# Wider opening tiles in the feed-forward phases, norms spread over three engines, and conv taps in another order, in a two-block transformer kernel

## The chip, the cores and the metric

The kernel runs on one core of a Trainium2 chip. The metric is the device time of one launch in microseconds (us), the median of several runs; less is better. The engines are named as in the profile: PE (TensorE matmuls; PEld its weight loads), DVE (VectorE), ACT (ScalarE), POOL (GpSimd) and SP (SyncE, which issues the transfers of weights).

## The reference, cut to what matters

Two models run one after the other on the same 256 tokens of width 1024, in fp32. Each has two layers.

```python
# first block, two layers
h = rms_norm(x, norm_mix_w);  z = h @ w_in + b_in
...                           # dilated attention, mLSTM, gates
x = x + mixed @ w_out
x = x + jnp.square(jax.nn.relu(rms_norm(x, norm_mlp_w) @ w_ff1)) @ w_ff2
# then a final rms_norm, then the second block, two layers
x = x + 0.5 * rmsnorm(swiglu_ffn(rmsnorm(x, ffn1_pre_g), ffn1_w_gu, ffn1_w_down), ffn1_post_g)
x = x + rmsnorm(mixing_sublayer(rmsnorm(x, mix_pre_g), ...), mix_post_g)
x = x + 0.5 * rmsnorm(swiglu_ffn(rmsnorm(x, ffn2_pre_g), ffn2_w_gu, ffn2_w_down), ffn2_post_g)

def rmsnorm(x, g):            # over 1024 columns
    return x * lax.rsqrt(jnp.mean(x * x, -1, keepdims=True) + EPS) * g
def swiglu_ffn(h, w_gu, w_down):
    a, b = jnp.split(h @ w_gu, 2, axis=-1)
    return (jax.nn.silu(a) * b) @ w_down
```

The mixing sublayer of the second block has four branches. Two matter here: a causal convolution over 256 channels with 31 taps and a layer norm behind it (the mean over channels comes out of a matmul), and a sparse attention that keeps the 64 best keys of each query.

## The kernel before, in words

**Phases.** The program is a list of steps in ten phases: mix1, ff, mix1, ff (first block; ff is the relu feed-forward), then f1, mix2, f2, f1, mix2, f2 (second block; f1 and f2 are the silu feed-forwards). The 256 tokens are two halves of 128, called token 0 and token 1 (`t`).

**Products.** Every fp32 operand is split into a high and a low part, and each product is three matmuls (high by high, high by low, low by high), all recorded on line 184. Weights come in tiles of 1 MB: SP issues the transfer (L210), ACT casts the high part (L224, two halves), DVE subtracts for the low part (L233, two halves), and PE multiplies. Three raw tiles, five high and four low ones can be in flight. A step uses one tile, 12288 columns of moving operand. Where weights are the stationary operand, matmuls are 512 and 256 columns wide (the low part of the tokens is joined by L348 on ACT and L349 on DVE, which free the PSUM bank); where tokens are stationary they are as wide as the tile's columns. PSUM has four banks for such products (`wk`) and four for the rest (`acc`).

**Seams.** Between two phases (`seam`) the norm of token 0 is made while token 1 still runs its last steps, and the norm of token 1 while token 0 opens the next phase. At such a place ACT squares the two 512-column halves with a sum each (L469), POOL makes the reciprocal root in three operations (L462, L463, and the power L464), DVE scales (L477), PE transposes (L358), and ACT and DVE split the result (L301, L302). Where a phase ends with a norm of its own (f1, mix2, f2: `post_residual`) there are two such chains in a row: squares of the sums in PSUM, POOL, then on DVE `y = acc * r * w` (L503) and `x = 0.5 * y + x` (L505) or `x = y + x` (L507) for each half, and then the norm that the next phase begins with.

**Openings.** A feed-forward phase opens with tokens as the stationary operand, so that token 0 can start before token 1: with relu three blocks of 256 columns for each token, with silu two blocks, each a pair of 256-column tiles (`start`), all over the full depth of 1024. The products of a block are transposed later (`tail`). The other blocks (`full`) have weights as the stationary operand.

**Side work.** The branches of mix2 are generators. After each step every generator goes on to its next `yield`. A scheduler orders each engine's queue at build time by priority and modelled readiness: the conv has low priority (−60), norms have high priority (120).

Of the kernel before, what the change touches and what calls it, by code (L numbers as in the profile page):

```python
# [12 lines left out]
AF = mybir.ActivationFunctionType  # L13
OP = mybir.AluOpType
# [3 lines left out]
P = 128  # L18
# [104 lines left out]
class Net:  # L123
# [334 lines left out]
    def rstd_halves(self, ss):  # L458

        nc = self.nc  # L460
        m0, m1, r = self.tiny(1), self.tiny(1), self.tiny(1)
        nc.gpsimd.tensor_scalar(out=m0, in0=ss[0], scalar1=1.0 / D, scalar2=EPS, op0=OP.mult, op1=OP.add)  # L462
        nc.gpsimd.tensor_scalar(out=m1, in0=ss[1], scalar1=1.0 / D, scalar2=m0, op0=OP.mult, op1=OP.add)  # L463
        nc.gpsimd.tensor_tensor(out=r, in0=m1, in1=self.mhalf[:, 0:1], op=OP.pow)  # L464
        return r

    def square(self, junk, src):
        ss = self.tiny(1)
        self.nc.scalar.activation(junk, src, AF.Square, accum_out=ss)  # L469
        return ss  # L470
# [26 lines left out]
    def post_residual(self, t, accs, w, half):  # L497

        nc = self.nc
        y = self.slot([P, D])  # L500
        r = self.rstd_halves([self.square(y[:, cs], accs[t][h]) for h, cs in enumerate(HALF)])
        for h, cs in enumerate(HALF):
            nc.vector.scalar_tensor_tensor(out=y[:, cs], in0=accs[t][h], scalar=r, in1=w[:, cs], op0=OP.mult, op1=OP.mult)  # L503
            if half:
                nc.vector.scalar_tensor_tensor(out=self.x[t][:, cs], in0=y[:, cs], scalar=0.5, in1=self.x[t][:, cs], op0=OP.mult, op1=OP.add)  # L505
            else:
                nc.vector.tensor_add(self.x[t][:, cs], y[:, cs], self.x[t][:, cs])  # L507

# [98 lines left out]

    def ff_plan(self, tag, w1, w2, kind, head):

        nc = self.nc  # L610
        n = (D_FF if kind == "relu" else D_FF_2) // 256
        nw = 1 if kind == "relu" else 2
        act, held = {}, {}
# [8 lines left out]
        def first_tiles(i):  # L622
            if kind == "relu":
                return (self.w_tile(w1, i * 256),)
            return (self.w_tile(w1, i * 256), self.w_tile(w1, D_FF_2 + i * 256))

        def tail(i, t, g):
            def gen():
                b = self.bank([P, 2, P])
                for k in range(2):  # L630
                    self.turn(b[:, k, :], g[:, k * P : (k + 1) * P])
                ts = tok(t)
                self.split(act[i].his(0, ts), act[i].los(0, ts), b)
                return
                yield
            return gen()

        def start(i, t, j):
            def fn(w):
                if i not in act:  # L640
                    act[i] = XT(self, 2)
                if j == 0:
                    held[t] = self.bank([P, nw, 256])
                b = held[t]
                self.a_mm([b[:, j, :]], self.xt, 0, t, w, 8, True, True, 256)
                self.flush()
                if j < nw - 1:
                    return
                g = self.slot([P, 2, 256])
                if kind == "relu":  # L650
                    nc.scalar.activation(g[:, 0, :], b[:, 0, :], AF.Relu)
                    nc.vector.tensor_mul(g[:, 1, :], g[:, 0, :], g[:, 0, :])
                else:
                    nc.scalar.activation(g[:, 0, :], b[:, 0, :], AF.Silu)
                    nc.vector.tensor_mul(g[:, 1, :], b[:, 1, :], g[:, 0, :])
                self.late.append(tail(i, t, g[:, 1, :]))
            return fn
# [29 lines left out]

        tiles = [first_tiles(i) for i in range(head)]
        starts = [[(start(i, t, j), (tiles[i][j],)) for i in range(head) for j in range(nw)] for t in range(2)]
        ntail = TAIL  # L690
# [375 lines left out]
    def mix2_plan(self, l):  # L1066
# [125 lines left out]
        def conv():  # L1192
            pt, hb = st["pt"], st["hb"]
            cv = self.half([P, 2, T])
            n = 0
            for c in range(2):
                for k in range(CONV_K):
                    w = pt[:, 2 * k + c : 2 * k + c + 1]
# [5 lines left out]
                    if n % TAPS == 0:  # L1204
                        yield
            yield
            b = self.acc([P, T])
# [54 lines left out]
        def sparse():  # L1262
# [3 lines left out]
            for t in (1, 0):  # L1266
# [130 lines left out]
    def plan(self):  # L1397
# [10 lines left out]
        def make(kind, l):  # L1408
            if kind == "mix1":
                return self.mix1_plan(l)  # L1410
            if kind == "ff":
                return (None, *self.ff_plan("ff", a["w_ff1"][l], a["w_ff2"][l], "relu", 3))
# [3 lines left out]
            return (None, *self.ff_plan(kind, a[f"{n}_w_gu_2"][l], a[f"{n}_w_down_2"][l], "silu", 2))  # L1416

# [114 lines left out]
```

## Time and profile before

| | before |
|---|---|
| time, median of 3 runs | 2001.76 us (2001.09 to 2002.98) |
| profiled execution, its own time | 2001.08 us |
| its span | 1999.3 us |
| mean granted TensorE clock in it | 0.994 |
| PE busy | 1944.3 us (97%) |
| DVE busy | 1321.1 us (66%) |
| ACT busy | 1029.2 us (51%) |
| POOL busy | 63.6 us (3%) |

The span is what the trace shows; the time of the run has 1.8 us around it. PE is busy nearly all the time, so a change is worth what it takes from PE's own work and from the few places at which PE waits.

### The profile page before, as it was taken

Reading aid. Unit: us, or ns where it says so; the run is one execution under the profiler, and the core shown is the slowest. Engines: PE = TensorE matmul, PEld = TensorE weight load, DVE = VectorE, ACT = ScalarE, POOL = GpSimd, SP = SyncE. Lnnn points to the kernel's source line nnn. Section 1 sums busy time; section 2 is a strip of 40 time slices with the busy share of each in tenths; the row PEclk is TensorE's granted clock in tenths of the full one; section 3 lists DMA queues with packets and bytes.
Section 4 is the critical chain, followed back from the end, with each engine's and each line's share of the span. In section 5 each row is a group of like instructions: output and inputs, shape, how many; then the busy total and the mean of one; then the engine's idle time right before and its main releaser. Section 6 shows DMA issues by size and latency. Waiting matters only on the chain.

```text
span 1999.3 us, 27988 instructions
## 1 busy us (share of the span) xinstructions
PE 1944.3 (97%) x11208; PEld 1687.3 (84%) x11208; DVE 1321.1 (66%) x2070; ACT 1029.2 (51%) x1694; POOL 63.6 (3%) x147
## 2 busy tenths in 40 slices
PE   7999999999999999999999999999999999999998
PEld 5888888888888888988798888888888798888887
DVE  5866666577666656655669777556655669777554
ACT  5555444455645444555555455555555555455552
POOL 0000000000000000000100000000000100000000
PEclk8999999999999999999999999999999999999999
DMA  8554565555445565556555455555556444546551
GB/s 282 164 175 140 166 209 190 190 191 174 142 158 181 189 196 175 196 189 213 162 153 160 157 179 201 190 198 177 191 188 214 154 148 154 162 174 206 190 194 70
DMA packets 252911, 356.97 MB, mean 179 GB/s; under 512 B 9399, under 2 KB 206188, under 8 KB 252780
## 3 DMA queue, kind: packets, MB, share of 16 engines
q1 hardware_dynamic: 252780, 355.17, 53.9%
q8 instruction: 88, 1.44, 0.3%
q14 instruction: 43, 0.35, 0.1%
HBM read 353.31 MB, written 1.84 MB: 178 GB/s over the span
## 4 chain that ended last, share of the span: by engine, by line
PE 86%; DVE 6%; ACT 3%; issue 2%; POOL 1%; DMA 1%; SPq 0%; POOLq 0%; DVEq 0%; ACTq 0%
PE wk L184 51%; PE acc L184 30%; DVE lo L233 2%; PE wk L358 1%; ACT slot L469 1%; ACT hi L224 1%; PE acc L358 1%; DVE half L1202 1%; DVE slot L477 1%; DMA raw<-in_w_in_dram 1%; DVE slot L503 1%; POOL tiny L464 1%; DMA raw<-in_w_ff_dram 1%; POOL tiny L463 1%; PE acc L834 0%
## 5 line engine op out<-in xcount | busy, mean ns | idle before, releaser
L184 PE MATMUL wk<-slot,hi 128*128 128x512 f32 (+1 forms) x3424 | 1022.3, 363 | 3.0 <-ACT slot L301 3.0
L233 DVE TENSOR_TENSOR lo<-raw,hi 128x1024 fp32r<-128x1024 f32 (+1 forms) x646 | 775.7, 1218 | 303.6 <-PE wk L184 212.1
L224 ACT CAST hi<-raw 128x1024 fp32r<-128x1024 f32 (+1 forms) x646 | 651.6, 1049 | 290.6 <-PE acc L184 114.2
L184 PE MATMUL wk<-slot,lo 128*128 128x256 f32 x2880 | 763.7, 282 | 0.0
L184 PEld LDWEIGHTS wk<-slot,hi 128*128 128x128 f32 x3424 | 597.7, 190 | 87.4 <-ACT slot L301 3.4
L184 PE MATMUL acc<-hi,slot 128*128 128x512 f32 x1920 | 617.0, 394 | 3.4 <-ACT slot L301 2.2
L184 PEld LDWEIGHTS wk<-slot,lo 128*128 128x128 f32 x2880 | 547.6, 190 | 24.7
L184 PEld LDWEIGHTS acc<-hi,slot 128*128 128x128 f32 x1920 | 362.3, 189 | 80.0 <-ACT slot L301 2.9
L184 PE MATMUL acc<-lo,slot 128*128 128x512 f32 x960 | 377.4, 393 | 0.0
L184 PEld LDWEIGHTS acc<-lo,slot 128*128 128x128 f32 x960 | 181.5, 189 | 37.3
L348 ACT COPY slot<-wk 128x256 f32<-128x256 f32 x196 | 73.2, 374 | 268.1 <-PE wk L184 267.7
L349 DVE TENSOR_TENSOR slot<-wk,slot 128x256 f32<-128x256 f32 x196 | 82.7, 422 | 106.8 <-ACT slot L348 106.8
L184 PE MATMUL wk<-hi,slot 128*128 128x256 f32 x704 | 134.6, 288 | 5.4 <-DVE slot L302 3.9
L184 PEld LDWEIGHTS wk<-hi,slot 128*128 128x128 f32 x704 | 111.3, 191 | 8.6 <-DVE slot L302 5.7
L184 PE MATMUL wk<-lo,slot 128*128 128x256 f32 x352 | 99.2, 283 | 0.0
L348 ACT COPY half<-wk 128x256 f32<-128x256 f32 x96 | 35.5, 370 | 87.0 <-PE wk L184 86.8
L302 DVE TENSOR_TENSOR slot<-slot 128x512 fp32r<-128x512 f32 x62 | 42.9, 692 | 41.3 <-ACT slot L301 41.3
L301 ACT CAST slot<-wk 128x256 fp32r<-128x256 f32 x108 | 38.0, 374 | 58.6 <-PE wk L358 50.1
L184 PEld LDWEIGHTS wk<-lo,slot 128*128 128x128 f32 x352 | 67.3, 191 | 0.2
L301 ACT CAST slot<-slot 128x512 fp32r<-128x512 f32 x62 | 38.6, 623 | 51.0 <-DVE slot L674 31.3
L358 PE MATMUL wk<-ident,slot 128*128 128x128 f32 x216 | 39.9, 281 | 19.7 <-DVE slot L477 12.9
L1202 DVE SCALAR_TENSOR_TENSOR half<-slot,prmT,half 128x256 f32<-128x256 f32 x120 | 57.3, 483 | 0.2
(238 smaller groups left out, 1040.2 us busy)
## 6 DMA issues: line engine op xcount, KB each, us to landing
raw<-in_w_in_dram SPq DMA_DIRECT2D x90, 1024.0 KB
raw<-in_ffn_w_gu_dram SPq DMA_DIRECT2D x88, 1024.0 KB
raw<-in_w_ff_dram SPq DMA_DIRECT2D x64, 1024.0 KB
raw<-in_ffn_w_down_dram SPq DMA_DIRECT2D x44, 1024.0 KB
raw<-in_w_out_dram SPq DMA_DIRECT2D x16, 1024.0 KB
raw<-in_w_branch_dram SPq DMA_DIRECT2D x8, 1024.0 KB
raw<-in_w_proj_att_dram SPq DMA_DIRECT2D x4, 1024.0 KB
raw<-in_w_proj_mlstm_dram SPq DMA_DIRECT2D x4, 1024.0 KB
```

Source lines behind the costliest of these rows:

```text
L184: i = self.nc.tensor.matmul(*args, **kwargs)
L224: nc.scalar.copy(his[j][:, p], raw[j][:, p])
L233: nc.vector.tensor_sub(lo[:, p], r[:, p], hi[:, p].bitcast(F32))
L301: nc.scalar.copy(hi, src)
L302: nc.vector.tensor_sub(lo, src, hi.bitcast(F32))
L348: self.nc.scalar.copy(dst, b[:, 1, :])
L349: self.nc.vector.tensor_add(dst, b[:, 0, :], dst)
L358: self.nc.tensor.transpose(dst, src, self.ident[: src.shape[0], : src.shape[0]])
L463: nc.gpsimd.tensor_scalar(out=m1, in0=ss[1], scalar1=1.0 / D, scalar2=m0, op0=OP.mult, op1=OP.add)
L464: nc.gpsimd.tensor_tensor(out=r, in0=m1, in1=self.mhalf[:, 0:1], op=OP.pow)
L469: self.nc.scalar.activation(junk, src, AF.Square, accum_out=ss)
L1202: nc.vector.scalar_tensor_tensor(out=cv[:, c, :], in0=hb[:, c, k : k + T], scalar=w, in1=cv[:, c, :], op0=OP.mult, op1=OP.add)
```

## The change

Five things change. The feed-forward phases open with tiles of 512 columns and half the depth (two groups of two such tiles for each token; with relu that is four blocks of 256, one more than before; with silu each tile holds 256 columns of both matrices, loaded by two transfers). In `rstd_halves` DVE makes the first sum, ACT the second, and POOL only the power; the squares carry the factor 1/1024 as a scale of 1/32. In `post_residual` the weight, and the 0.5, are multiplied in before `r` is known, and `x = y * r + x` is all that follows it; the squares write to a buffer of their own. The conv's taps alternate its two channel blocks, and there is one more yield behind them. The sparse attention has one more yield behind its exponentials.

```diff
     def rstd_halves(self, ss):
-        nc.gpsimd.tensor_scalar(out=m0, in0=ss[0], scalar1=1.0 / D, scalar2=EPS, op0=OP.mult, op1=OP.add)
-        nc.gpsimd.tensor_scalar(out=m1, in0=ss[1], scalar1=1.0 / D, scalar2=m0, op0=OP.mult, op1=OP.add)
+        nc.vector.tensor_scalar(out=m0, in0=ss[0], scalar1=EPS, scalar2=None, op0=OP.add)
+        nc.scalar.activation(m1, ss[1], AF.Identity, bias=m0)
         nc.gpsimd.tensor_tensor(out=r, in0=m1, in1=self.mhalf[:, 0:1], op=OP.pow)
     def square(self, junk, src):
-        self.nc.scalar.activation(junk, src, AF.Square, accum_out=ss)
+        self.nc.scalar.activation(junk, src, AF.Square, scale=1.0 / 32.0, accum_out=ss)
     def post_residual(self, t, accs, w, half):
-        y = self.slot([P, D])
-        r = self.rstd_halves([self.square(y[:, cs], accs[t][h]) for h, cs in enumerate(HALF)])
+        y, junk = self.slot([P, D]), self.slot([P, D])
+        ss = []
         for h, cs in enumerate(HALF):
-            nc.vector.scalar_tensor_tensor(out=y[:, cs], in0=accs[t][h], scalar=r, in1=w[:, cs], op0=OP.mult, op1=OP.mult)
-            if half:
-                nc.vector.scalar_tensor_tensor(out=self.x[t][:, cs], in0=y[:, cs], scalar=0.5, in1=self.x[t][:, cs], op0=OP.mult, op1=OP.add)
-            else:
-                nc.vector.tensor_add(self.x[t][:, cs], y[:, cs], self.x[t][:, cs])
+            ss.append(self.square(junk[:, cs], accs[t][h]))
+            nc.vector.scalar_tensor_tensor(out=y[:, cs], in0=accs[t][h], scalar=0.5 if half else 1.0, in1=w[:, cs], op0=OP.mult, op1=OP.mult)
+        r = self.rstd_halves(ss)
+        for h, cs in enumerate(HALF):
+            nc.vector.scalar_tensor_tensor(out=self.x[t][:, cs], in0=y[:, cs], scalar=r, in1=self.x[t][:, cs], op0=OP.mult, op1=OP.add)
     def ff_plan(self, tag, w1, w2, kind):
+        nw, per = (1, 2) if kind == "relu" else (2, 1)
+        head = 2 * per
+        def start_tile(i, half):
+            if kind == "relu":
+                return self.z_tile(w1, i * 512, half)
+            rows = w1[half * 512 : half * 512 + 512]
+            loads = []
+            for j, c in enumerate((i * 256, D_FF_2 + i * 256)):
+                loads.append((lambda r, j=j: r[:, :, j * 256 : (j + 1) * 256], rows[:, c : c + 256].rearrange("(k p) n -> p k n", p=P)))
+            return self.weight([P, 4, 512], *loads)
...
-                if j == 0:
-                    held[t] = self.bank([P, nw, 256])
+                if half == 0:
+                    held[t] = self.bank([P, 512])
                 b = held[t]
-                self.a_mm([b[:, j, :]], self.xt, 0, t, w, 8, True, True, 256)
+                self.a_mm([b], self.xt, 4 * half, t, w, 4, half == 0, half == 1)
                 self.flush()
...
-        starts = [[(start(i, t, j), (tiles[i][j],)) for i in range(head) for j in range(nw)] for t in range(2)]
+        starts = [[(start(i, t, half), (tiles[i][half],)) for i in range(2) for half in range(2)] for t in range(2)]
...
         def conv():
-            for c in range(2):
-                for k in range(CONV_K):
+            for k in range(CONV_K):
+                for c in range(2):
...
                     if n % TAPS == 0:
                         yield
+            yield
             yield
             b = self.acc([P, T])
             for c in range(2):
                 nc.tensor.matmul(b, lhsT=self.mean, rhs=cv[:, c, :], start=c == 0, stop=c == 1)
...
         def sparse():
                     nc.scalar.activation(lg[:, h, :], lg[:, h, :], AF.Exp, bias=nb[:, h : h + 1], accum_out=l[:, h : h + 1])
                 yield
+                yield
                 pT = self.slot([P, 4, t + 1, P])
```

The order of instructions on three engines shows how this moves work. Line numbers of the changed kernel are its own.

**DVE, the end of the conv in mix2.** The taps are L1202 before and L1217 after; the row behind the mean's matmuls, which subtracts the mean, is L1210 before and L1226 after. Before:

```order
L1202 SCALAR_TENSOR_TENSOR half<-slot,prmT,half 128x256
L233 TENSOR_TENSOR lo<-raw,hi 128x1024
L349 TENSOR_TENSOR half<-wk,half 128x256
L1202 SCALAR_TENSOR_TENSOR half<-slot,prmT,half 128x256 x2
L233 TENSOR_TENSOR lo<-raw,hi 128x1024
L1202 SCALAR_TENSOR_TENSOR half<-slot,prmT,half 128x256
L349 TENSOR_TENSOR half<-wk,half 128x256
L1202 SCALAR_TENSOR_TENSOR half<-slot,prmT,half 128x256
L233 TENSOR_TENSOR lo<-raw,hi 128x1024
L1202 SCALAR_TENSOR_TENSOR half<-slot,prmT,half 128x256 x2
L1210 TENSOR_TENSOR half<-half,acc 128x512
```

After:

```order
L1217 SCALAR_TENSOR_TENSOR half<-slot,prmT,half 128x256 x2
L233 TENSOR_TENSOR lo<-raw,hi 128x1024
L349 TENSOR_TENSOR half<-wk,half 128x256
L233 TENSOR_TENSOR lo<-raw,hi 128x1024
L302 TENSOR_TENSOR slot<-acc,slot 128x2x256
L233 TENSOR_TENSOR lo<-raw,hi 128x1024
L349 TENSOR_TENSOR half<-wk,half 128x256
L233 TENSOR_TENSOR lo<-raw,hi 128x1024 x2
L349 TENSOR_TENSOR half<-wk,half 128x256
L1226 TENSOR_TENSOR half<-half,acc 128x512
```

Before, taps stand one by one between the casts right up to L1210; after, five casts, three joins and a split of other work stand between the last two taps and L1226. In the stretch ahead of this piece the taps of the changed kernel stand in runs of up to five.

**ACT, token 1 at the seam from f1 to mix2.** The squares are L469 before and L470 after, L463 is the second sum of `rstd_halves` in the changed kernel, and the table load (L1119, L1134) belongs to the opening of mix2. Before:

```order
L301 CAST slot<-wk 128x2x128
L469 ACTIVATE slot,tiny<-acc 128x512 x2
L224 CAST hi<-raw 128x1024 x2
L469 ACTIVATE slot,tiny<-x_64 128x512 x2
L1119 ACT_TABLE_LOAD
L1119 ACTIVATE slot<-acc 128x512
```

After:

```order
L301 CAST slot<-wk 128x2x128 x3
L470 ACTIVATE slot,tiny<-acc 128x512 x2
L224 CAST hi<-raw 128x1024 x2
L463 ACTIVATE tiny<-tiny 128x1
L470 ACTIVATE slot,tiny<-x_64 128x512 x2
L463 ACTIVATE tiny<-tiny 128x1
L1134 ACT_TABLE_LOAD
L1134 ACTIVATE slot<-acc 128x512
```

The second sum of the post-norm stands behind two weight casts that it has nothing to do with; before, this sum was on POOL and behind nothing.

**PE, token 0 in the opening of the f2 phase behind the first mix2**, around the transposes of token 1's norm (eight of the ten L358; the other two belong to a `tail`). Before:

```order
L184 MATMUL wk<-lo,slot 128x256
L184 MATMUL wk<-hi,slot 128x256
L358 MATMUL wk<-ident,slot 128x128 x10
L184 MATMUL wk<-hi,slot 128x256
L184 MATMUL wk<-lo,slot 128x256
L184 MATMUL wk<-hi,slot 128x256 x2
```

After:

```order
L184 MATMUL wk<-hi,slot 128x512 x2
L184 MATMUL wk<-lo,slot 128x512
L358 MATMUL wk<-ident,slot 128x128 x10
L184 MATMUL wk<-hi,slot 128x512 x2
L184 MATMUL wk<-lo,slot 128x512
L184 MATMUL wk<-hi,slot 128x512 x2
```

The matmuls are twice as wide and half as many. Counted in steps of 12288 columns, the transposes stood 1.62 steps behind the start of token 0's opening and stand 1.96 steps behind it now, with 0.04 steps of token 0 left behind them. In mix2, counted in the same way on PE, two steps instead of one stand between the scores of the sparse attention and the transposes of its exponentials, and the mean's matmuls of the conv stand one step later.

## Rows read from the trace of the kernel before

**Rows 1.** The page: busy time of the engines; shares of the chain by engine.

```profile
PE 1944.3 (97%) x11208; PEld 1687.3 (84%) x11208; DVE 1321.1 (66%) x2070; ACT 1029.2 (51%) x1694; POOL 63.6 (3%) x147
...
PE 86%; DVE 6%; ACT 3%; issue 2%; POOL 1%; DMA 1%; SPq 0%; POOLq 0%; DVEq 0%; ACTq 0%
```

**Rows 2.** Waits of PE, whole run: total us, times, longest us.

```profile
PE wk L358 <- DVE slot L477: 12.9, 8, 7.6
PE acc L1209 <- DVE half L1202: 7.7, 2, 3.8
...
PE wk L358 <- DVE slot L655: 4.1, 4, 1.4
PE wk L184 <- DVE slot L302: 3.9, 4, 1.0
PE acc L358 <- ACT slot L1284: 3.4, 2, 1.9
PE acc L358 <- DVE slot L784: 3.3, 1, 3.3
```

**Rows 3.** The chain, one tile's matmuls in three forms: start us, us, what.

```profile
260.03 5.63 PE wk L184 x32
265.67 5.45 PE acc L184 x24
...
1220.84 5.75 PE wk L184 x48
```

**Rows 4.** Timeline of PE, first mix2, the conv's mean: idle before and releaser in brackets.

```profile
1119.56 0.59 PE L1209 MATMUL acc<-half,mean 128*128 128x256 f32 x2
1123.98 0.70 PE L1209 MATMUL acc<-half,mean 128*128 128x256 f32 x2 [3.83 <-DVE half L1202]
```

**Rows 5.** Stretches: length; busy us of PE, PEld, DVE, ACT, POOL; PEclk; DMA; GB/s.

```profile
1065.00:1124.00 59.00, 53.46 (x334) 45.99 (x332) 56.71 (x118) 35.94 (x64) 0.00 (x0) 1.00 0.58 181
...
1125.00:1128.50 3.50, 3.50 (x13) 2.96 (x12) 0.41 (x1) 0.63 (x1) 0.00 (x0) 0.51 0.74 253
1128.50:1132.00 3.50, 3.50 (x23) 3.09 (x22) 0.77 (x2) 0.48 (x2) 0.00 (x0) 1.00 0.02 5
1725.80:1729.30 3.50, 3.50 (x14) 3.02 (x13) 0.20 (x1) 0.63 (x1) 0.00 (x0) 0.51 0.69 241
1674.60:1678.10 3.50, 3.50 (x13) 3.02 (x14) 3.50 (x7) 3.50 (x6) 0.00 (x0) 0.51 0.64 246
39.60:49.90 10.30, 10.30 (x24) 6.68 (x23) 3.26 (x6) 4.05 (x7) 0.00 (x0) 0.50 0.79 252
```

**Rows 6.** Timeline of PE, both mix2 phases: transposes of the sparse attention's exponentials.

```profile
1073.89 1.92 PE L358 MATMUL acc<-ident,slot 128*128 128x128 f32 x8 [1.55 <-ACT slot L1284]
1673.02 2.08 PE L358 MATMUL acc<-ident,slot 128*128 128x128 f32 x8 [1.89 <-ACT slot L1284]
```

**Rows 7.** Timeline of DVE, first mix2, a cast near the conv's end.

```profile
1119.53 1.23 DVE L233 TENSOR_TENSOR lo<-raw,hi 128x1024 fp32r<-128x1024 f32 x1 [0.26 <-PE wk L184]
```

**Rows 8.** Groups by line and form: count, busy us, mean ns, idle before and releaser.

```profile
L1202 DVE SCALAR_TENSOR_TENSOR half<-slot,prmT,half 128x256 f32<-128x256 f32 x120 | 57.3, 483 | 0.2
...
L464 POOL TENSOR_TENSOR tiny<-tiny,mhalf 128x1 f32<-128x1 f32 x34 | 18.8, 552 | 2.8
...
L469 ACT ACTIVATION_READ_ACCUMULATOR slot<-x 128x1 f32 x44 | 8.4, 191 | 0.0
```

**Rows 9.** Timeline of ACT, POOL and DVE at the seam from mix2 to f2.

```profile
1195.00 0.19 ACT L469 ACTIVATION_READ_ACCUMULATOR slot<-x 128x1 f32 x1
...
1197.47 1.42 DVE L477 SCALAR_TENSOR_TENSOR slot<-x,tiny,slot 128x512 f32<-128x512 f32 x2 [0.80 <-POOL tiny L464]
...
1207.38 2.00 ACT L224 CAST hi<-raw 128x1024 fp32r<-128x1024 f32 x2 [0.56 <-DMA raw<-in_ffn_w_gu_dram]
...
1207.92 1.41 DVE L503 SCALAR_TENSOR_TENSOR slot<-acc,tiny,slot 128x512 f32<-128x512 f32 x2 [0.89 <-POOL tiny L464]
```

**Rows 10.** The chain, five transposes that wait for nothing.

```profile
1004.93 0.51 PE acc L358 x5
```

More of the change, by code (lines that the diff above doesn't have):

```diff
@@ L605, in w_step, with ff_plan @@
         self.step(fn, tile_)
-    def ff_plan(self, tag, w1, w2, kind, head):
+    def ff_plan(self, tag, w1, w2, kind):
         nc = self.nc
         n = (D_FF if kind == "relu" else D_FF_2) // 256
-        nw = 1 if kind == "relu" else 2
+        nw, per = (1, 2) if kind == "relu" else (2, 1)
+        head = 2 * per
         act, held = {}, {}
@@ L625, in first_tiles @@
             return (self.w_tile(w1, i * 256), self.w_tile(w1, D_FF_2 + i * 256))
+        def start_tile(i, half):
[6 more added lines that the diff above has]
+            return self.weight([P, 4, 512], *loads)
         def tail(i, t, g):
             def gen():
-                b = self.bank([P, 2, P])
-                for k in range(2):
+                b = self.bank([P, 2 * per, P])
+                for k in range(2 * per):
                     self.turn(b[:, k, :], g[:, k * P : (k + 1) * P])
                 ts = tok(t)
-                self.split(act[i].his(0, ts), act[i].los(0, ts), b)
+                for j in range(per):
+                    self.split(act[i + j].his(0, ts), act[i + j].los(0, ts), b[:, 2 * j : 2 * j + 2])
                 return
@@ L636, in tail, with start @@
             return gen()
-        def start(i, t, j):
+        def start(n, t, half):
+            i = n * per
             def fn(w):
-                if i not in act:
-                    act[i] = XT(self, 2)
-                if j == 0:
-                    held[t] = self.bank([P, nw, 256])
+                for j in range(per):
+                    if i + j not in act:
+                        act[i + j] = XT(self, 2)
+                if half == 0:
+                    held[t] = self.bank([P, 512])
                 b = held[t]
-                self.a_mm([b[:, j, :]], self.xt, 0, t, w, 8, True, True, 256)
+                self.a_mm([b], self.xt, 4 * half, t, w, 4, half == 0, half == 1)
                 self.flush()
-                if j < nw - 1:
+                if half == 0:
                     return
-                g = self.slot([P, 2, 256])
+                g = self.slot([P, 1024])
                 if kind == "relu":
-                    nc.scalar.activation(g[:, 0, :], b[:, 0, :], AF.Relu)
-                    nc.vector.tensor_mul(g[:, 1, :], g[:, 0, :], g[:, 0, :])
-                else:
-                    nc.scalar.activation(g[:, 0, :], b[:, 0, :], AF.Silu)
-                    nc.vector.tensor_mul(g[:, 1, :], b[:, 1, :], g[:, 0, :])
-                self.late.append(tail(i, t, g[:, 1, :]))
+                    nc.scalar.activation(g[:, 0:512], b, AF.Relu)
+                    nc.vector.tensor_mul(g[:, 512:1024], g[:, 0:512], g[:, 0:512])
+                else:
+                    nc.scalar.activation(g[:, 0:256], b[:, 0:256], AF.Silu)
+                    nc.vector.tensor_mul(g[:, 512:768], b[:, 256:512], g[:, 0:256])
+                self.late.append(tail(i, t, g[:, 512:1024]))
             return fn
@@ L686, in down @@
             return fn
-        tiles = [first_tiles(i) for i in range(head)]
-        starts = [[(start(i, t, j), (tiles[i][j],)) for i in range(head) for j in range(nw)] for t in range(2)]
+        tiles = [[start_tile(i, half) for half in range(2)] for i in range(2)]
+        starts = [[(start(i, t, half), (tiles[i][half],)) for i in range(2) for half in range(2)] for t in range(2)]
         ntail = TAIL
@@ L1411, in make @@
             if kind == "ff":
-                return (None, *self.ff_plan("ff", a["w_ff1"][l], a["w_ff2"][l], "relu", 3))
+                return (None, *self.ff_plan("ff", a["w_ff1"][l], a["w_ff2"][l], "relu"))
             if kind == "mix2":
@@ L1415, in make @@
             n = "ffn1" if kind == "f1" else "ffn2"
-            return (None, *self.ff_plan(kind, a[f"{n}_w_gu_2"][l], a[f"{n}_w_down_2"][l], "silu", 2))
+            return (None, *self.ff_plan(kind, a[f"{n}_w_gu_2"][l], a[f"{n}_w_down_2"][l], "silu"))
         pre_w = {"mix1": "norm_mix_w", "ff": "norm_mlp_w", "f1": "ffn1_pre_g_2", "mix2": "mix_pre_g_2", "f2": "ffn2_pre_g_2"}
```

## Prediction, made before the changed kernel ran

> **What bounds the kernel now.** I began with the page [rows 1]. PE is busy for 1944.3 of 1999.3 us, and the chain that ended last is PE for 86%. So there are two kinds of gain: cheaper work on PE, and the 55 us in which it does nothing. DVE at 66% and ACT at 51% matter only where PE waits for them.
>
> The list of PE's waits comes next [rows 2]. The reader should see that each of the large ones has one place. 7.7 us are two waits of the conv's mean (L1209) for the last taps (L1202). 3.4 us are the sparse attention's transposes waiting for exponentials (L1284). 3.3 us (L784) and the single 7.6 in the first row stand at the start of the run. The rest, 5.3 (12.9 less 7.6) for L477, 4.1 for L655 and 3.9 for L302, stand at the seams: 13.3 us.
>
> The chain in order of time gives the price of a tile by its form [rows 3]. The same 12288 columns take 5.75 us as 48 matmuls of 256, 5.63 as 32 of both widths, and 5.45 as 24 of 512.
>
> Last I looked at what follows a wait, in stretches with the granted clock [rows 5]. It is 0.51 of 2.4 GHz, the lower level of 1.2, for 3.5 us behind each of the two conv means and behind the second sparse wait, and 0.50 for 10.3 us in the start. Ahead of each, PE had idled.
>
> **Openings.** With relu, an opening has 4 x 12288 columns for both tokens: three times that in three blocks of 256 and the fourth block in the mixed form. 3 x 5.75 + 5.63 = 22.88 us becomes 4 x 5.45 = 21.80, so −1.08 in each of two phases. With silu 4 x 5.75 = 23.00 becomes 21.80, −1.20 in each of four. Together **−7.0 us** [rows 3]. The form that replaces them, tokens stationary and 512 moving columns, is the one of the 5.45 row, so I take it whole. These matmuls are PE's own work in a chain that is PE, and nothing hides them.
> The Trainium skill, "TensorE: Matmul & The Clock Gate", section "Back-to-back issue gap", speaks against this: an isolated matmul at full clock costs its columns at 2.4 GHz plus 2.5 ns. By that the 544 matmuls that go (80 in each relu phase, 96 in each silu phase) would give 1.4 us, not 7.0. Our rows differ from it: 24 matmuls fewer save 0.30 us, 12.5 ns each, and the rows decide.
>
> **Waits in mix2.** In a mix2 phase the first mean matmul stands at 1119.56 and the second at 1123.98 [rows 4]; unhindered it would be 0.3 us behind the first, so 4.1 us are lost, in two phases 8.2. In the changed order the mean stands one step later on PE (5.63 us, more than the 4.1), and on DVE the last taps have five casts, three joins and a split behind them before the subtraction. Both make them early, so I count all of it. The exponentials' eight transposes cost 1.55 of wait and 1.92 of their own, where five that wait for nothing take 0.51 and so eight take 0.82 [rows 6, 10]: 2.65 lost, and in the second phase 1.89 + 2.08 − 0.82 = 3.15. They too stand a step later now, which covers both. Then the clock: at 0.51 a stretch of 3.5 us holds 13 matmuls, at 1.00 it holds 23 [rows 5]; ten matmuls at 0.15 are 1.5 us, three times 4.5. Sum 8.2 + 5.8 + 4.5 = **−18.5 us**. If the clock falls all the same, −14.0.
> The cover for this is the lead of the casts. From 1065 to 1124 DVE is busy for 56.7 of 59.0 us and PE for 53.5 [rows 5], so without its waits PE runs faster there than DVE. But near the end of it a cast still waits for PE to free a buffer [rows 7], so casts are as far ahead as four low tiles allow; after 1125 DVE is busy for only 0.41 and 0.77 of 3.5 us. A lag of 56.7 − 53.5 = 3.2 us is less than one step and is paid out of that lead.
> The same page, section "What's actually happening", says that half clock is the default and that activity releases it. The trace agrees: 0.51 right behind idle stretches, and 1.00 one stretch later.
>
> **Seams.** From the last sum's end at 1195.19 to DVE's start at 1197.47 POOL's three operations took 2.3 us [rows 9]. Now POOL has only the power, 0.55 [rows 8]. The trace has no 128x1 addition on ACT; the nearest rows are a sum's read-out, 0.19 [rows 8], below, and POOL's power itself, 0.55 [rows 8], above. I take 0.25, since the read-out is the nearer row, on the same engine, and with hand-overs 1.0 for the chain: up to −1.3. The first scaling of the post-norm, two operations of 1.41 us, no longer follows `r`: −1.3, as what is left costs about 0.1 more.
> Against this stands the queue. At token 1 of the post seams the second sum now stands behind two casts that wait for a transfer: they end at 1207.38 + 2.00 = 1209.38, and DVE, which began at 1207.92, can begin at about 1210.3 [rows 9]. That is +2.4, less the 1.3: h of token 1 comes about 1.1 us later. Its transposes also stand later on PE, 1.96 steps behind the opening instead of 1.62, which is 1.9 us, but only 0.04 steps of token 0 are left to cover its splits. So token 1 gains nothing and token 0 gains most of its share. Of the 13.3 us [rows 2] I take a third: **−4.3 us**. Bounds: −10 (three quarters go) and +4 (token 1 loses 1.1 at six seams, 6.6, and token 0 gives back 2.6). The wider start helps here, since its first half asks for four of the eight splits.
>
> **Start and end.** In the changed order the six transposes that wait 3.3 us for L784 [rows 2] stand behind the little matmuls (L450). The copy that those need is itself close behind, so I take **−1.5** of the 3.3 (bounds 0 and −3.3; another −5.1 if the 10.3 us at half clock [rows 5] go too, which I don't count, as PE still idles there). At the end of the run nothing covers the last post-norm: its first scaling goes, **−1.4**, by the same pair of 1.41 [rows 9] (bounds −0.5 and −2.7). What alternating taps may save each lies on DVE under PE, and the 16 more transfer issues on SP's queue under its lead: nothing.
>
> **Sum.** −7.0 − 18.5 − 4.3 − 1.5 − 1.4 = −32.7 on the profiled execution's own 2001.08: 1968.4. The median of the runs is 0.7 above that execution, so **1969 us**.
>
> **Rivals.**
> Seams turn worse (chance 0.15): the seam term is +4 and token 1's splits, uncovered, add 0.7 at six seams, so 1969 + 8.3 + 4.2, about 1981. For it speaks the wait of 0.56 ahead of the two casts; against it that transfers start when a cast frees a raw buffer, and these casts move earlier.
> The start's half clock goes too (0.08): 1964.
> The openings pay 1.4 and not 7.0 (0.05), if it is not the width that makes the 5.45 row short but that another operand moves: 1975. Against it, both rows have tokens stationary in 128-column pieces and differ in width alone.
> The change doesn't do what it says in mix2 (0.06): DVE is the true bound there, and PE then waits for casts or joins for as long as it did for taps. The −18.5 stay, 1987.
> Slower (0.06 for the mechanism): the taps in runs of five. A tap is 0.48 us [rows 8], so a run holds up a cast or join behind it by 2.4 us instead of 0.48, 1.9 more; some 20 runs in both phases are 38 us. It decides where DVE is the bound, so that the 18.5 stay as well: 1987 plus the exposed part of 38, which is slower from half of it (19 us) on, and 2025 with all of it. Against it stand four banks and four low tiles with 5.6 us a step.
>
> **How the numbers follow.** The forecast has 0.60, with its own range of 1961 to 1977 (mix2 −14 to −19, seams −7 to 0, start and end −1 to −6). The range of 8 in 10 takes in 1964, 1975 and the seams' 1981 and reaches toward 1987: 1959 to 1985. A measurement of this kernel can tell 0.2% from no change, 4 us. Faster 0.60 + 0.15 + 0.08 + 0.05 + 0.06 = 0.94, less 0.02 for what no rival names; the last case gives 0.04 within 0.2% with that, and 0.04 slower.
>
> **What would show it.** In the changed profile the conv's mean and the exponentials' transposes should be gone from PE's waits, and PEclk should be 1.00 throughout mix2. A silu opening should show 24 matmuls in 5.45 us. At the seams POOL should show only L464 in a norm, and DVE's first operation behind the post-norm's `r` at token 1 should wait for ACT's casts. The forecast is wrong if waits for L349, L302 or L233 appear inside mix2, if token 1's waits at the seams grow past 2 us each, or if the 512-wide tiles come out near 5.7 us.

## The result and the profile after

The changed kernel takes 1967.23 us (median of four runs, 1964.74 to 1968.07) against 2001.42 (2000.89 to 2002.98): the ratio is 0.9826, 95% interval 0.9809 to 0.9843. The forecast was 1969 in 1959 to 1985. The profiled execution took 1968.07 us, 33.0 less than that of before, so the terms can be checked one by one in its trace.

The page of the changed kernel, span and busy time:

```profile
span 1966.3 us, 26882 instructions
...
PE 1932.1 (98%) x10672; PEld 1655.8 (84%) x10672; DVE 1322.0 (67%) x2096; ACT 1034.5 (53%) x1722; POOL 39.9 (2%) x79
```

PE has 12 us less to do than in [rows 1]; the rest of the 33.0 is idle time that has gone. Its waits, in the form of [rows 2]:

```profile
PE wk L358 <- DVE slot L478: 12.0, 7, 7.7
PE wk L358 <- DVE slot L670: 3.7, 4, 1.1
PE wk L184 <- ACT slot L301: 3.0, 2, 1.5
PE wk L450 <- DVE slot L441: 2.7, 1, 2.7
...
PE wk L184 <- DVE slot L302: 1.2, 2, 0.7
...
PE wk L358 <- DVE slot L667: 0.6, 1, 0.6
...
PE acc L184 <- DVE slot L302: 0.4, 1, 0.4
```

Three more rows of the list of before, beside [rows 2]:

```profile
PE wk L184 <- ACT slot L301: 4.2, 4, 1.5
...
PE wk L358 <- DVE slot L652: 1.9, 2, 1.0
PE acc L184 <- DVE slot L302: 1.2, 2, 0.6
```

The conv's mean and the exponentials' transposes are missing from the list: these were 7.7 and 3.4 us. L302 is 1.2 instead of 3.9 in the openings (`wk`). L670 is the old L655, L478 the old L477 and L667 the old L652; the first two have lost little. At the start L784's 3.3 us have gone, and 2.7 for L441 have come.

To see where the time came from, take the same matmuls in both traces. In the timeline of PE the second branch's product (L1179, now L1194) opens the side work of each mix2 phase, and the matmul that spreads the conv's scale (L1224, now L1240) nearly ends it. Before:

```profile
1021.91 1.03 PE L1179 MATMUL acc<-half,pw 128*128 128x256 f32 x4
...
1138.20 0.61 PE L1224 MATMUL acc<-ident,tiny 128*128 128x128 f32 x4
...
1620.70 1.03 PE L1179 MATMUL acc<-half,pw 128*128 128x256 f32 x4
...
1738.73 0.61 PE L1224 MATMUL acc<-ident,tiny 128*128 128x128 f32 x4
```

After:

```profile
1018.31 1.03 PE L1194 MATMUL acc<-half,pw 128*128 128x256 f32 x4
...
1132.05 0.60 PE L1240 MATMUL acc<-ident,tiny 128*128 128x128 f32 x4
...
1601.55 1.03 PE L1194 MATMUL acc<-half,pw 128*128 128x256 f32 x4
...
1715.24 0.61 PE L1240 MATMUL acc<-ident,tiny 128*128 128x128 f32 x4
```

The second of each pair now stands one step, 5.6 us, later on PE, which has to be added to what was saved between the two. From the first to the second, 116.29 us became 113.74 in the first mix2 phase and 118.03 became 113.69 in the second: 8.2 and 9.9 saved, 18.1 together. Ahead of the first marker 3.6 us are saved, between the phases 482.50 less 469.50 less the step, 7.4, and behind the last marker the remaining 3.9.

### The profile page after: what moved, and what is told of

Its sections match the earlier page's. It is cut to its first block, busy times and chain, and to the rows that moved or that the text cites. A ratio compares the mean times of both kernels' runs of the same rounds, so it can differ in the third digit from the quotient of the medians.

```text
span 1966.3 us, 26882 instructions
## 1 busy us (share of the span) xinstructions
PE 1932.1 (98%) x10672; PEld 1655.8 (84%) x10672; DVE 1322.0 (67%) x2096; ACT 1034.5 (53%) x1722; POOL 39.9 (2%) x79
## 5 line engine op out<-in xcount | busy, mean ns | idle before, releaser
L184 PE MATMUL wk<-slot,hi 128*128 128x512 f32 (+1 forms) x3392 | 1006.6, 362 | 3.0 <-ACT slot L301 3.0
L233 DVE TENSOR_TENSOR lo<-raw,hi 128x1024 fp32r<-128x1024 f32 (+1 forms) x646 | 775.3, 1217 | 294.2 <-PE wk L184 199.8
L184 PE MATMUL wk<-slot,lo 128*128 128x256 f32 x2848 | 754.0, 281 | 0.0
L184 PEld LDWEIGHTS wk<-slot,hi 128*128 128x128 f32 x3392 | 590.2, 190 | 85.3 <-ACT slot L301 3.4
L184 PEld LDWEIGHTS wk<-slot,lo 128*128 128x128 f32 x2848 | 540.0, 190 | 24.4
L349 DVE TENSOR_TENSOR slot<-wk,slot 128x256 f32<-128x256 f32 x192 | 80.9, 421 | 101.1 <-ACT slot L348 101.1
L184 PE MATMUL wk<-hi,slot 128*128 128x512 f32 x384 | 125.9, 398 | 1.4 <-DVE slot L302 1.2
L184 PEld LDWEIGHTS wk<-hi,slot 128*128 128x128 f32 x384 | 71.6, 188 | 18.4 <-DVE slot L302 3.5
L184 PE MATMUL wk<-lo,slot 128*128 128x512 f32 x192 | 75.5, 393 | 0.0
L302 DVE TENSOR_TENSOR slot<-slot 128x512 fp32r<-128x512 f32 x60 | 41.6, 693 | 40.6 <-ACT slot L301 40.6
L301 ACT CAST slot<-wk 128x256 fp32r<-128x256 f32 x112 | 39.6, 372 | 51.7 <-PE wk L358 44.2
L301 ACT CAST slot<-slot 128x512 fp32r<-128x512 f32 x60 | 37.3, 621 | 49.8 <-DVE slot L689 31.3
L358 PE MATMUL wk<-ident,slot 128*128 128x128 f32 x224 | 41.5, 285 | 17.1 <-DVE slot L478 12.0
L302 DVE TENSOR_TENSOR slot<-wk,slot 128x256 fp32r<-128x256 f32 x112 | 44.7, 420 | 16.2 <-ACT slot L301 15.3
L470 ACT ACTIVATE slot<-x 128x512 f32<-128x512 f32 x44 | 27.8, 633 | 51.2 <-DVE x L496 32.0
```

The costliest lines, as they stand in the source:

```text
L184: i = self.nc.tensor.matmul(*args, **kwargs)
L233: nc.vector.tensor_sub(lo[:, p], r[:, p], hi[:, p].bitcast(F32))
L301: nc.scalar.copy(hi, src)
L302: nc.vector.tensor_sub(lo, src, hi.bitcast(F32))
L349: self.nc.vector.tensor_add(dst, b[:, 0, :], dst)
L358: self.nc.tensor.transpose(dst, src, self.ident[: src.shape[0], : src.shape[0]])
```

## The experiments

The ratios are to runs of the kernel before on the same chip. Waits are quoted from each kernel's own list.

**The yields alone.** The two extra yields go into the kernel before, and the taps keep their order.

```diff
                     if n % TAPS == 0:
                         yield
+            yield
             yield
             b = self.acc([P, T])
...
                 yield
+                yield
                 pT = self.slot([P, 4, t + 1, P])
```

> The kernel before with the two extra yields in mix2 alone (one behind the conv's taps, one behind the sparse attention's exponentials); the taps keep their order. Theory A, that a later place on PE is what removes the waits: both the conv mean's and the exponentials' waits are gone from PE's list, the clock is 1.00 in mix2, and the time is 18 us below before, about 1983. Theory B, that the conv's wait goes because alternating taps are put earlier on DVE: only the sparse part goes (5.8 of wait and 1.5 of clock), the conv's mean still waits for the last taps, about 1994.

Measured: 1983.52 us (1982.87 to 1984.36), ratio 0.9906 (0.9892 to 0.9921), 19.0 below before. All its large waits are those of seams and start; the first two:

```profile
PE wk L358 <- DVE slot L477: 13.0, 8, 7.8
PE wk L184 <- ACT slot L301: 4.6, 4, 1.5
```

Theory A holds: both waits are gone, with the old order of taps. In the first mix2 phase the last tap now ends at 1122.29 and the mean starts at 1123.17:

```profile
1121.82 0.47 DVE L1202 SCALAR_TENSOR_TENSOR half<-slot,prmT,half 128x256 f32<-128x256 f32 x1
...
1123.17 1.02 PE L1210 MATMUL acc<-half,mean 128*128 128x256 f32 x4
```

**The taps alone.**

```diff
-            for c in range(2):
-                for k in range(CONV_K):
+            for k in range(CONV_K):
+                for c in range(2):
```

> The kernel before with the taps alternating between the channel blocks and no extra yield. Theory A: the mean stands where it stood and still waits, time within 3 us of 2001. Theory B: the last taps are done before PE comes to the mean, the conv's 8.2 us of wait and 3.0 of clock go, about 1990, and the sparse attention's wait of 2.65 and 3.15 us stays. The slower rival, that runs of five taps hold up casts and joins, would show as waits of PE for lines 233 or 349 inside mix2 and a time above 2005.

Measured: 1991.13 us (1989.05 to 1992.01), ratio 0.9941 (0.9924 to 0.9957), 11.4 below. Its waits:

```profile
PE acc L358 <- ACT slot L1284: 3.6, 2, 1.9
```

The conv's wait is gone here too, without a yield, while the sparse attention's stays. So theory A of this run falls: either edit is enough for the conv. The taps now stand in runs of up to five on DVE, and the last two end at 1120.88, 1.0 us before the mean starts:

```profile
1120.01 0.87 DVE L1202 SCALAR_TENSOR_TENSOR half<-slot,prmT,half 128x256 f32<-128x256 f32 x2
...
1121.88 1.02 PE L1209 MATMUL acc<-half,mean 128*128 128x256 f32 x4
```

There is no wait for L233 or L349 inside mix2: the slower rival of the prediction has no trace in this run.

**The changed kernel with the old order of taps.** The diff above, reversed, in the changed kernel.

> The changed kernel with the conv's taps in their old order (one channel block after the other), both extra yields kept. Theory A, that the yields alone remove mix2's waits and the taps' order is then worth nothing: within 2 us of the changed kernel, no wait for the taps among PE's waits. Rival, that without PE's other waits DVE falls behind and the early taps are needed: the mean waits again, 1970 or more.

Measured: 1966.22 us (1963.15 to 1968.25), ratio 0.9821 (0.9808 to 0.9835), against 0.9822 for the changed kernel on another chip (below). Beside the yields the order of taps is worth nothing that can be measured. Together these three runs settle the mix2 term: the waits came from positions in queues, of the mean and the transposes on PE and of the last taps on DVE, and moving either one is enough for the conv.

**The openings alone.** `ff_plan` as changed, all else as before (its diff is shown with the change).

> The kernel before with the 512-column openings alone. Theory A, that width pays as the rows of before say: 24 matmuls of an opening in 5.45 us, 7.0 us in all, and 1 to 3 more at the seams because the first half asks for four splits only: 1992 to 1995. Rival, that a matmul fewer saves 2.5 ns: 1.4 us, about 2000.

Measured: 1987.96 us (1986.61 to 1989.82), ratio 0.9929 (0.9914 to 0.9944), 14.6 below: twice the 7.0 of the width, and more than I expected. Its waits at the seams:

```profile
PE wk L358 <- DVE slot L669: 4.7, 4, 1.5
...
PE wk L184 <- DVE slot L302: 1.4, 2, 0.8
```

L302, token 0's splits, fell from 3.9 to 1.4 with the norms untouched, L301 from 4.2 to 3.0, and L652 (1.9, the first relu block's squares) is gone, while L669 (the old L655) rose by 0.6: −5.0 at the seams. The tile of half depth asks for half of the splits, and waits less for them. Its profiled execution has a span of 1986.7 us, 12.6 less than before: 5.0 of it at the seams leave 7.6 for the openings themselves, where 7.0 were forecast. PE's own busy time fell by 6.6, from the 1944.3 of [rows 1]:

```profile
PE 1937.7 (98%) x10672; PEld 1656.9 (83%) x10672; DVE 1319.1 (66%) x2062; ACT 1026.7 (52%) x1688; POOL 63.7 (3%) x147
```

Width and half depth come in one edit. That the first pays in PE's own work and the second in the waits is read from these lists; no run has one without the other. (In this trace a half-clock stretch came behind the first sparse wait and not behind the second, so they cancel.)

**The norms alone.** `rstd_halves`, `square` and `post_residual` as changed, all else as before.

> The kernel before with the changed norms alone (sums on DVE and ACT, the weight multiplied in first, a buffer of its own for the squares). Theory A, that token 0 gains and token 1 loses what it gains to ACT's casts: 1 to 3 us at the seams and 1.4 at the end, 1997 to 1999, and behind token 1's sums the second sum stands on ACT behind two casts. Rival, that the norms bring all of what the seams gained: 6 us or more, 1995 or less. Rival, that the queue on ACT costs more than the shorter chain gives: 2002 or more.

Measured: 1994.96 us (1991.39 to 1995.69), ratio 0.996 (0.9945 to 0.9975), 7.6 below. The first rival is nearest. But one wait grew:

```profile
PE wk L358 <- DVE slot L653: 4.3, 2, 2.4
```

L653 is the old L652: 1.9 us in two waits became 4.3, at the seams from mix1 to ff, where no post-norm is shortened and only the sums have moved.

**The post-norm's order alone.** Of the norms' change only `post_residual`; sums and power stay on POOL.

```diff
     def post_residual(self, t, accs, w, half):
-        y = self.slot([P, D])
-        r = self.rstd_halves([self.square(y[:, cs], accs[t][h]) for h, cs in enumerate(HALF)])
+        y, junk = self.slot([P, D]), self.slot([P, D])
...
+        r = self.rstd_halves(ss)
```

> The kernel before with the reordered post-norm alone (weight multiplied in first, squares to a buffer of their own), all sums and the power on POOL as before. Theory A, that the shorter path behind the root is what the norms' part gains and the move of the sums off POOL gains nothing or costs: at least as fast as the kernel with all the changed norms (7.6 us below before), 1992 to 1995. Rival, that the two halves of the norms' change share the gain: 1996 to 2000.

Measured: 1991.62 us (1990.02 to 1992.14), ratio 0.995 (0.9937 to 0.9964), 9.9 below. Its waits:

```profile
PE wk L358 <- DVE slot L477: 8.4, 3, 7.8
...
PE wk L358 <- DVE slot L655: 2.1, 4, 0.8
```

L477 fell from 12.9 to 8.4, of which 7.8 stand at the start, and L655 from 4.1 to 2.1. One half of the norms' change does all of its work, token 1 included, and the other half (sums off POOL) takes some of it back: 9.9 against 7.6, on two chips and with intervals that overlap. The next runs test that in the changed kernel.

**Where the sums are made.** Four kernels on one chip: the changed one again, both sums in one DVE operation, both sums on POOL, and, with the DVE sum, the start's copy on POOL.

```diff
-        nc.vector.tensor_scalar(out=m0, in0=ss[0], scalar1=EPS, scalar2=None, op0=OP.add)
-        nc.scalar.activation(m1, ss[1], AF.Identity, bias=m0)
+        nc.vector.scalar_tensor_tensor(out=m1, in0=ss[0], scalar=EPS, in1=ss[1], op0=OP.add, op1=OP.add)
```

```diff
-        nc.vector.tensor_scalar(out=m0, in0=ss[0], scalar1=EPS, scalar2=None, op0=OP.add)
-        nc.scalar.activation(m1, ss[1], AF.Identity, bias=m0)
+        nc.gpsimd.tensor_scalar(out=m0, in0=ss[0], scalar1=EPS, scalar2=None, op0=OP.add)
+        nc.gpsimd.tensor_scalar(out=m1, in0=ss[1], scalar1=1.0, scalar2=m0, op0=OP.mult, op1=OP.add)
```

```diff
-        nc.vector.tensor_copy(rows, rb.unsqueeze(2).to_broadcast([33, 4, P]))
+        nc.gpsimd.tensor_copy(rows, rb.unsqueeze(2).to_broadcast([33, 4, P]))
```

> The changed kernel once more, on the same chip as the three kernels beside it: 1965 to 1968.

> The changed kernel with both sums of a norm in one operation on DVE (ss0 + EPS + ss1) and the power on POOL; ACT has no part of it. Theory A, that ACT's second sum behind two casts is what holds up token 1 at the post seams (it ran 2.7 us after the squares were done, and DVE's operation behind the power waited 1.96 us): the sum runs right behind the first scaling on DVE, 1.2 us earlier, at five seams where PE waits 1.1 to 2.0 us: 3 to 5 us below the changed kernel, about 1963. Rival, that the chain of token 1 is held up elsewhere (squares, scaling, transposes) or that token 0 loses as much behind DVE's own casts: within 2 us of the changed kernel.

> The changed kernel with both sums back on POOL, all else as changed. If leaving only the power on POOL is what brings the seams' gain, the chain of three operations (2.3 us under DVE's casts, against 1.0) returns: 5 us or more above the changed kernel, 1972 or more. If it is the queue on ACT that matters at token 1 and the length of POOL's chain at token 0, the two cancel: within 2 us of the changed kernel. If POOL's chain is the better place altogether: 1964 or less.

> The kernel with both sums on DVE, and the copy of the bias rows at the start (which the little matmuls wait 2.7 us for, on DVE behind a cast and the rotary operations) on POOL. Theory A: the copy is done long before, the wait of 2.7 us goes, and with it perhaps the half clock of the 10 us behind it (5 us): 2.5 to 7.5 us below the kernel with both sums on DVE. Rival, that the wait only moves to the transposes behind the little matmuls, which wait for the rotary operations: no change.

| kernel | median us (range) | ratio (95% interval) |
|---|---|---|
| changed, again | 1966.41 (1965.17 to 1968.24) | 0.9822 (0.9808 to 0.9835) |
| both sums in one DVE operation | 1965.43 (1964.57 to 1966.23) | 0.9815 (0.9802 to 0.9828) |
| both sums on POOL | 1963.69 (1963.19 to 1964.34) | 0.9808 (0.9794 to 0.9821) |
| DVE sum, start's copy on POOL | 1965.96 (1964.46 to 1967.05) | 0.9818 (0.9805 to 0.9832) |

With the sums back on POOL the time is 2.7 us lower, and the slowest of its four runs is faster than the fastest of the changed kernel beside it. The clock at the start is not the reason: from 39 to 50 us the granted clock of its profiled execution is 0.50, and 0.56 in the changed kernel's (its row stands further below, under the start). Its waits:

```profile
PE wk L358 <- DVE slot L478: 8.2, 3, 7.6
PE wk L184 <- DVE slot L302: 3.3, 4, 1.0
```

In the changed kernel beside it these are 11.8 and 1.1: token 1 gains more than token 0 loses. The timeline at the seam from mix2 to f2, token 1, shows why. The changed kernel (its first profiled execution), ACT, POOL and DVE in order of time:

```profile
1193.03 0.21 ACT L470 ACTIVATION_READ_ACCUMULATOR slot<-acc 128x1 f32 x1
1193.83 2.00 ACT L224 CAST hi<-raw 128x1024 fp32r<-128x1024 f32 x2 [0.58 <-DMA raw<-in_ffn_w_gu_dram]
1195.73 0.29 ACT L463 ACTIVATE tiny<-tiny 128x1 f32<-128x1 f32 x1
1196.09 0.55 POOL L464 TENSOR_TENSOR tiny<-tiny,mhalf 128x1 f32<-128x1 f32 x1 [11.08 <-ACT tiny L463]
1196.68 1.42 DVE L508 SCALAR_TENSOR_TENSOR x<-slot,tiny,x 128x512 f32<-128x512 f32 x2 [1.96 <-POOL tiny L464]
```

The same place with the sums on POOL:

```profile
1189.31 0.21 ACT L470 ACTIVATION_READ_ACCUMULATOR slot<-acc 128x1 f32 x1
...
1189.69 0.27 POOL L463 TENSOR_SCALAR tiny<-tiny 128x1 f32<-128x1 f32 x1 [0.20 <-ACT slot L470]
...
1190.86 1.40 DVE L508 SCALAR_TENSOR_TENSOR x<-slot,tiny,x 128x512 f32<-128x512 f32 x2
```

From the start of the last square's read-out to that of L508 it is 3.65 us in the first and 1.55 in the second, where L508 waits for nothing but DVE itself. ACT's second sum stands behind two casts that wait 0.58 us for a transfer, as the order said. The price, L302, is token 0's. The kernel with the DVE sum is 1.0 us below the changed one, too near it for a verdict, and not the 3 to 5 of theory A. By the lists it wins at token 1 (2.2 us instead of 4.3 in the rows of L670, there L669) and loses at the start, where PE waits 4.4 us instead of 2.7 for L441. With the copy on POOL the wait moved, as the rival said: PE then waited 4.7 us for the rotary operations (L798).

**Mixed sums, and the start.** Token 0's sums as changed, token 1's on POOL; then, on top, one more yield ahead of token 0's first transposes and of the little matmuls, with their copy on POOL.

```diff
-        nc.vector.tensor_scalar(out=m0, in0=ss[0], scalar1=EPS, scalar2=None, op0=OP.add)
-        nc.scalar.activation(m1, ss[1], AF.Identity, bias=m0)
+        if t == 0:
+            nc.vector.tensor_scalar(out=m0, in0=ss[0], scalar1=EPS, scalar2=None, op0=OP.add)
+            nc.scalar.activation(m1, ss[1], AF.Identity, bias=m0)
+        else:
+            nc.gpsimd.tensor_scalar(out=m0, in0=ss[0], scalar1=EPS, scalar2=None, op0=OP.add)
+            nc.gpsimd.tensor_scalar(out=m1, in0=ss[1], scalar1=1.0, scalar2=m0, op0=OP.mult, op1=OP.add)
```

```diff
             nc.vector.tensor_add(t2, m[:, 2], m[:, 3])
             yield
             yield
+            if t == 0 and l == 0:
+                yield
...
-        nc.vector.tensor_copy(rows, rb.unsqueeze(2).to_broadcast([33, 4, P]))
+        nc.gpsimd.tensor_copy(rows, rb.unsqueeze(2).to_broadcast([33, 4, P]))
         yield
+        yield
```

> The changed kernel with token 0's sums as changed (DVE and ACT) and token 1's sums on POOL. Theory A, that token 0 gains by the short chain under DVE's casts (with sums on POOL its splits wait 1.0 us at four seams) and token 1 loses by ACT's queue: the best of both, 1 to 3 us below the kernel with all sums on POOL, 1961 to 1963. Rival, that the two tokens' gains hide each other: 1964, as with all sums on POOL.

> The kernel before this one (token 0's sums as changed, token 1's on POOL) with the start changed: one more yield ahead of the transposes of token 0's rotated queries and keys in the first layer, one more ahead of the little matmuls, and the copy that these wait for on POOL. Theory A, that PE's wait of 3 us at the start goes and the clock stays at its upper level behind it: 3 to 8 us below the kernel with mixed sums, 1954 to 1959. Rival, that only the wait goes and the 10 us at half clock stay: 2 to 3 us. Rival, that the wait moves on to a matmul a few instructions later: no change.

Measured: mixed 1963.91 us (1962.49 to 1964.72), ratio 0.981 (0.9797 to 0.9824); with the start 1962.28 (1961.09 to 1962.63), ratio 0.9802 (0.9788 to 0.9815). Mixed sums are no better than all sums on POOL: theory A fell. By the two lists of waits the mixed kernel gains 1.7 us at L302 (3.3 to 1.6), and gives it back at the start (4.4 us for L441, where the kernel with all sums on POOL waits 3.3 for L799) and in the row of L478, there L482 (8.2 to 9.8). The second kernel is the fastest of this study by its median, 1.6 us below the first. Its start, transfer and copy of the bias, wait of PE and stretch with the clock:

```profile
31.33 0.33 SPq L439 DMA_DIRECT2D rb<-in_rel_bias_dram  x1
...
36.27 1.43 POOL L441 COPY slot<-rb 33x512 f32<-33x512 f32 x1 [19.48 <-DMA rb<-in_rel_bias_dram]
...
37.75 5.49 PE L451 MATMUL wk<-slot 33*128 33x384 f32 x8 [2.38 <-POOL half L872]
...
39.00:50.00 11.00, 11.00 (x35) 7.58 (x34) 5.98 (x12) 5.18 (x8) 0.00 (x0) 0.60 0.78 247
```

The transposes' wait is gone, and the little matmuls now wait 2.38 us for POOL. The row names a memset that ended last (L872), but their copy ends only at 37.70: it could not start before the transfer of the bias, issued at 31.33, had landed at about 36.27, and it takes 1.43 us on POOL, where it takes 0.41 on DVE. The clock stays low behind it. The rival that the wait moves on is the nearest.

## Why the prediction was right, point by point

The sum of −32.7 meets the 33.0 of the profiled execution. Three terms came out nearly as forecast. Two did not, the seams too small by about 2 us and the start too large by 1.5, and that these two nearly cancel is luck.

**Openings, −7.0: 6.6 to 7.6 by the kernel with the openings alone.** In the stretch of the changed kernel from one pair of transposes to the next, in the silu opening behind the first mix2, PE does 24 wide matmuls, with a pair of transposes about them:

```profile
1206.30:1211.84 5.54, 5.54 (x27) 4.54 (x26) 5.22 (x6) 4.54 (x6) 0.00 (x0) 1.00 0.40 132
```

That is 5.5 us for what took 5.75 as 48 matmuls [rows 3], against 5.69 if each of 24 matmuls fewer had saved 2.5 ns. The row decided rightly against the 2.5 ns that the prediction weighed it with. In the kernel with the openings alone PE's busy time fell by 6.6, and the span less the seams leaves 7.6.

**Mix2, −18.5: 18.1 in the trace, 19.0 with the yields alone.** Waits and clock were read from the right rows, and the cover held. The stretches from ahead of the exponentials' transposes to the end of the side work, in both phases, and the mean's matmuls and the transposes in the first, which now wait for nothing:

```profile
1060.00:1132.00 72.00, 72.00 (x463) 64.25 (x462) 67.21 (x138) 42.66 (x75) 1.80 (x2) 1.00 0.62 194
1643.00:1715.00 72.00, 72.00 (x463) 64.23 (x461) 67.37 (x139) 42.59 (x75) 1.80 (x2) 1.00 0.62 198
```

```profile
1074.24 1.04 PE L358 MATMUL acc<-ident,slot 128*128 128x128 f32 x8
...
1118.90 1.02 PE L1225 MATMUL acc<-half,mean 128*128 128x256 f32 x4
```

PE is busy for all of 72.0 us at full clock, and DVE for 67.2 and 67.4 of them. DVE was nearly as full as the rival said, and still no cast or join kept PE waiting, as the argument from the lead of the casts had it; the lead itself was not varied. I had counted both edits of the conv without asking what each does alone; the runs show that one would have done. The slower rival, runs of five taps, has nothing in the traces of the changed kernel and of the taps alone; the one wait of its kind is 0.5 us for a join (L349) in the kernel with the DVE sum.

**Seams, −4.3: measured between −6.0 and −6.8, mis-sized, and with one cause wrong.** Total 33.0 less 18.1 in mix2, less 1.3 at the end and 0.0 at the start, leaves 13.6 for openings and seams: 6.6 for the seams if the openings gave 7.0, and 6.0 if they gave 7.6. In the lists, the 13.3 us that the prediction started from lost 4.0 (0.9 for L477, 0.4 for L655, 2.7 for L302), close to the third that it took. The rest came from waits that the 13.3 had left out: 1.3 for L652, 1.2 for L301 and 0.8 for L302 ahead of mix2, less 0.5 that came new for L1186. That makes 6.8. (The bounds of this term count six seams behind a post-norm; the phases have five.)

That token 0 gains and token 1 hardly does was right, the relu openings (L652) aside: apart from the start's 7.7 and one wait of 0.65, the first two rows of the list are token 1's. L670 is a product of token 0, but it stands on DVE right behind token 1's scaling.

The failed step is the one that gave the short chain on POOL "up to −1.3". Moving the sums off POOL cost 2.7 us in the changed kernel, as the queue on ACT at token 1 outweighed what token 0 gained. What gained was the post-norm's order (9.9 us alone) and, which I had in one sentence without a number, the half depth of the opening tiles (5.0 at the seams). The parts don't add: 19.0, 14.6 and 7.6 alone make 41.2, the whole 34.2. One overlap is seen in the lists: openings alone and norms alone each take away most of L302's 3.9 us, which can only go once.

**Start, −1.5: came out as 0.** The step that failed is the half of the wait that was taken as gone because the little matmuls' copy is "close behind". The copy (L441) stands on DVE behind a cast and rotary operations, and PE's wait of 3.3 us became one of 2.7 a few instructions earlier:

```profile
38.42 5.46 PE L450 MATMUL wk<-slot 33*128 33x384 f32 x8 [2.69 <-DVE slot L441]
...
39.00:50.00 11.00, 11.00 (x30) 7.26 (x29) 4.34 (x8) 4.47 (x7) 0.00 (x0) 0.56 0.74 235
```

The queue on DVE is not all of it. The copy also needs the transfer of the bias, which SP issues at 32.16 here. In the kernel with the changed start the copy on POOL waited for that transfer, for 4.9 us after its issue. By the same 4.9 it lands near 37.1 here (an estimate), 0.8 us before the copy starts on DVE at 37.91. An earlier transfer was not tried.

**End, −1.4: 1.3.** The last matmul starts at 1959.69 in a span of 1966.3, before at 1991.39 in one of 1999.3: from there to the end 7.9 us became 6.6.

## What to carry to other kernels

A wait on the bounding engine that comes from its place in a queue is worth its whole length and the clock behind it; one yield in the program moved it, and no wait for a cast came in its place here, where casts run a few tiles ahead. Before a tiny operation is moved to an engine with a shorter operation, read what stands ahead of it there: 0.3 us of work on ACT started 2.5 us after its last input, behind two casts. Gains at one place don't add up, so time each part alone and look which wait both take away.

## What the runs showed of the hardware that was not expected

POOL's operations on 128x1 are not of one length, and the length goes with what DVE does. With sums on POOL, at the seam from mix2 to f2:

```profile
1177.03 1.22 DVE L233 TENSOR_TENSOR lo<-raw,hi 128x1024 fp32r<-128x1024 f32 x1
...
1177.29 1.03 POOL L462 TENSOR_SCALAR tiny<-tiny 128x1 f32<-128x1 f32 x1 [1.63 <-ACT slot L470]
...
1188.20 1.21 DVE L233 TENSOR_TENSOR lo<-raw,hi 128x1024 fp32r<-128x1024 f32 x1
...
1189.03 0.46 POOL L462 TENSOR_SCALAR tiny<-tiny 128x1 f32<-128x1 f32 x1 [8.87 <-ACT slot L470]
...
1192.89 0.22 POOL L462 TENSOR_SCALAR tiny<-tiny 128x1 f32<-128x1 f32 x1 [2.28 <-ACT slot L470]
```

The same operation takes 1.03 us when it begins early in a DVE cast that reads two SBUF tensors, 0.46 when it begins late in one, and 0.22 when DVE does nothing. In the first two cases it ends 0.07 and 0.08 us behind the end of the cast, as if it waited for that. In the trace of before, two of POOL's three operations in the gap of [rows 9], which took 0.94 and 1.12 us, begin inside such casts too. No run takes the cast away with all else the same. The Trainium skill, "GPSIMD Engine Reference", section "Specifications", says that GpSimd's SBUF interface is shared with VectorE and contended by DVE instructions with two SBUF inputs; these rows agree.

The half clock at the start is not the same in every execution of one program. In the profiled execution of the changed kernel with the old tap order, whose start has the same wait of 2.7 us for L441, the same stretch reads:

```profile
39.00:50.00 11.00, 11.00 (x58) 8.73 (x57) 7.47 (x17) 6.46 (x10) 0.00 (x0) 0.84 0.89 271
```

PE did 58 matmuls and transposes in it where it did 30 in the changed kernel's profiled execution, and this execution took 1963.15 us in a kernel whose runs reach 1968.25. Its mean granted clock over the whole run was 0.999, and 0.996 in the two runs of 1967.44 and 1968.25. The 3 to 5 us by which runs of one kernel differ here are of the size of this stretch, so gains of 1 us in this kernel need many runs.
